# A two-layer trunk on one core: the diagonal products of the linear attention in another order, and two empty steps in its schedule

## The chip, the cores and the metric

The kernel runs on one core of one Trainium2 chip. The metric is the device time of one execution, in microseconds; lower is better. The core's engines work side by side and each takes its instructions in order: TensorE (PE in the profile, with its weight loads as PEld), VectorE (DVE), ScalarE (ACT), GpSimd (POOL), and SyncE (SP), which issues the DMA transfers.

## The reference

The input is a stream of 2064 tokens of 1024 channels (16 learned ones and 2048 given ones). Layer 0 is a gated convolution module, layer 1 gated linear attention; after each comes `h = LayerNorm(sqrt(2)·h + mixer(h))`. All is float32. Of layer 1, which the change touches:

```python
u = h @ w_in                       # q, k: 4 heads x 128;  v, r: 4 heads x 256;  a1: 16
glog = log_sigmoid(a1 @ w_a2 + b_a) / 16
# per head, in chunks; bc is the running sum of glog inside a chunk
att[t, s] = sum_d q[t,d] k[s,d] exp(bc[t,d] - bc[s,d])     for s <= t
o = att @ v + (q * exp(bc)) @ S
S = exp(b_last) * S + (k * exp(b_last - bc)).T @ v
o = o * rsqrt(mean(o*o) + 1e-6) * norm_g
y = (o * silu(r)) @ w_out
```

## The kernel before, in words

The program has four phases. Phases 1 and 2 are the convolution layer, phase 3 is the attention, phase 4 its output projection and the last LayerNorm. Wide matrix products are made as three float32r products of high and low parts (`mm3`, lines 102 to 108).

Phase 3 (`phase3`, line 798) works through four blocks of 512 tokens (the first also holds the 16 learned ones) and, in each, four heads. For each head two things are woven together.

- The **projections** (`proj_units`, line 555): k, q, v and the two halves of r, as TensorE products named `pj_b<block><k|q|v|r>`, with weights that SyncE fetches and ACT and DVE split. After each unit the generator yields its cost: 1 for a product of 512 columns by 128 channels (24 matmuls), 0.53 for each of four v chunks, 0.5 for the gates (`gates`, line 626, which end in the running sum `b` on DVE, line 643).
- The **attention** of the head (`gla_units`, line 651), a generator of steps between `yield`s: the decayed keys `kh` and queries; the transposes of the keys (`pk`, line 691); the levels m = 64, 32, 16 of the attention matrix (`att`, line 727) with the state updates (`ds`, lines 704 and 705); the levels 8, 4, 2 and 1, whose factors `A` are built by POOL, ACT and DVE (lines 717 to 721, 741 to 744); the diagonal products `sm` (lines 755 and 756); their masking, sum and split into `a_h` and `a_l` (lines 758 to 768); the outputs `o` (line 777); their norm; and the transposes of the outputs (`oT`, line 789), which leave for `og_d`.

The diagonal products are small. A head's block has four chunks of 128 tokens, taken two by two into one PSUM tile `sm`; each chunk has four blocks of 32 tokens at rows s = 0, 32, 64, 96. For each block there are four products with 128 rows of contraction: levels 8, 4 and 2, each 32 x 32, and one of 32 x 48 that holds level 1 and the diagonal. The rows s to s + 32 of the output fix which 32 columns of the array a product takes.

How many attention steps are run per projection unit is set by `GRATE` (line 40): `debt += GRATE * cost`, and one step for each whole unit of debt (lines 806 to 809). A head's steps run while the r of this head and the k, q and v of the next are projected: 2 + 1 + 0.5 + 1 + 4 x 0.53 = 6.62 units of cost. A head has 14 yields (15 in the first block). What is left of a head's steps is run out before the next head begins (lines 810 to 813). Steps and units only give the order in which the program is written: a scheduler then places the instructions on each engine by its own estimate of when they are ready, so their final order is not the written one.

Of the kernel before, what the change touches and what calls it, by code (L numbers as in the profile page):

```python
# [19 lines left out]
P = 128  # L20
# [16 lines left out]
NH = 4  # L37
TAU = 16.0
QSCALE = 128.0 ** -0.5
GRATE = 2.35  # L40
VCOST = 0.53
CB = 4
WRB = 3
# [6 lines left out]
class Trunk:  # L50
# [600 lines left out]
    def gla_units(self, h, hd, bi, t0, n):  # L651
        nc, K = self.nc, self
# [20 lines left out]
        bs, ks, qs = b[:, sl], k_[:, sl], q_[:, sl]  # L673
# [11 lines left out]
        nc.vector.tensor_tensor(kh, kh, ks, op=ALU.mult)  # L685
        nc.vector.tensor_tensor(ebf, ebf, qs, op=ALU.mult)
        qh, ql = self.pair3("q", eb, nc.gpsimd, nm)
        yield
        pt = self.pt.tile([P, 4, P], F32, tag="g", name=f"pk{nm}")
        for c in range(4):  # L690
# [20 lines left out]
        for m in (64, 32, 16, 8, 4, 2):  # L711
# [11 lines left out]
            if m >= 16:  # L723
                for c in range(4):
                    for s in range(0, P, 2 * m):
                        a = c * P + s
                        nc.tensor.matmul(
                            att[s : s + m, c, s + m : s + 2 * m],
                            lhsT=A[:, a : a + m],
                            rhs=A[:, a + m : a + 2 * m],  # L730
                            start=False,
                            stop=False,
                            skip_group_check=True,
# [4 lines left out]
        A1 = self.gp.tile([P, 16, 48], F32, tag="A1", name=f"A1{nm}", bufs=1)  # L738
# [8 lines left out]
        red = self.gp.tile([P, 4, 32], F32, tag="red", name=f"red{nm}")  # L747
        for c2 in range(2):
            sm = self.pt.tile([P, 2, 144], F32, tag="g", name=f"sm{nm}_{c2}")
            for c in range(2):  # L750
                for s in range(0, P, 32):
                    a = (2 * c2 + c) * P + s
                    w = slice(a, a + 32)
                    for i, m in enumerate((8, 4, 2)):
                        nc.tensor.matmul(sm[s : s + 32, c, 48 + 32 * i : 80 + 32 * i], lhsT=lv[m][:, w], rhs=lv[m][:, w], start=True, stop=True, skip_group_check=True)  # L755
                    nc.tensor.matmul(sm[s : s + 32, c, :48], lhsT=ks[:, w], rhs=A1[:, a // 32], start=True, stop=True, skip_group_check=True)
            ms = self.gp.tile([P, 2, 144], F32, tag="ms", name=f"ms{nm}_{c2}")
            nc.vector.tensor_tensor(ms, sm, K.lmask.unsqueeze(1).to_broadcast([P, 2, 144]), op=ALU.mult)
            rd = red[:, 2 * c2 : 2 * c2 + 2]
            nc.vector.tensor_reduce(rd, ms[:, :, 16:].rearrange("p c (l t) -> p c t l", t=32), axis=mybir.AxisListType.X, op=ALU.add)  # L760
            odd = rd.rearrange("p c (s u) -> p c s u", u=2)[:, :, :, 1]
            nc.vector.tensor_tensor(odd, odd, ms[:, :, :16], op=ALU.add)
            yield
# [2 lines left out]
            nc.vector.tensor_tensor(at[:, c], red[:, c].unsqueeze(1).to_broadcast([P, 4, 32]), K.blk, op=ALU.mult)  # L766
        nc.vector.tensor_tensor(at, at, att.rearrange("p c (a b) -> p c a b", b=32), op=ALU.add)
        ath, atl = self.pair3("a", at.rearrange("p c a b -> p c (a b)"), nc.gpsimd, nm, 1)
        yield
        osb = self.gp.tile([P, 4, 256], F32, tag="osb", name=f"osb{nm}", bufs=1)  # L770
        sq = self.gp.tile([P, 3, 4], F32, tag="sq", name=f"sq{nm}")
# [26 lines left out]
    def phase3(self, wo):  # L798
# [3 lines left out]
        for bi, h, cost, hd in self.proj_units():  # L802
            if bi > cur:
                cur = bi
                nb = self.block(bi + 1) if bi < last else self.load_half(wo, 0)
            debt += GRATE * cost
            while debt >= 1:
# [145 lines left out]
```

## Time and profile before

| | |
|---|---|
| median of 3 runs | 1757.4 us (1753.49 to 1759.08) |
| the profiled execution | 1755.36 us, of which its span is 1753.6 us |
| PE busy | 1702.3 us (97%), 11715 instructions |
| DVE busy | 1402.4 us (80%) |
| POOL, ACT busy | 944.3 us (54%), 842.9 us (48%) |
| granted TensorE clock, mean | 0.993 |

The span runs from the first instruction of the program to the last. A matmul's duration in the profile is its time through a pipeline, so the next one begins before it ends; what a product costs TensorE is the time from its start to the next start. A program matmul on plain float32 operands stands in the trace as two MATMUL records: the program has 1024 `sm` products, the trace 2048 records. The stretch from 820 to 1580 us holds the attention of all 16 heads.

### The profile page before, as it was taken

How to read it: one execution, taken by the hardware profiler on the slowest of the kernel's cores; microseconds unless marked ns; L12 is line 12 of the kernel's file. 1: busy time of each engine (PE TensorE's matmuls, PEld its weight loads, DVE VectorE, ACT ScalarE, POOL GpSimd, SP SyncE). 2: the span in 40 equal slices, each digit the busy share in tenths (PEclk: the TensorE clock that was granted, in tenths of full speed). 3: DMA queues.
4: the chain of work that ended last, by engine and by line, in shares of the span. 5: the costliest groups of instructions: out<-in, count | busy, mean ns of one | idle time of the engine just before them, and what ended most of it. 6: DMA issues, size and time to landing. Idle time of an engine off the chain costs nothing.

```text
span 1753.6 us, 29029 instructions
## 1 busy us (share of the span) xinstructions
PE 1702.3 (97%) x11715; PEld 1514.2 (86%) x11715; DVE 1402.4 (80%) x1869; ACT 842.9 (48%) x1269; POOL 944.3 (54%) x675
## 2 busy tenths in 40 slices
PE   8999999999998998999999999999999999999998
PEld 8999999999998776767888888888888878888886
DVE  5789999999998898777666687777878687887665
ACT  6445555655544454445455455555555455541000
POOL 0879999999975788756233233333333153331000
PEclk9999999999999999999999999999999999999999
DMA  7111111111256544433113222232223322354441
GB/s 244 37 37 37 37 69 40 73 56 54 75 169 217 173 162 139 140 124 99 67 61 109 87 92 78 84 105 79 85 85 96 111 73 85 123 165 162 147 135 62
DMA packets 103910, 178.72 MB, mean 102 GB/s; under 512 B 8624, under 2 KB 68400, under 8 KB 103776
## 3 DMA queue, kind: packets, MB, share of 16 engines
q1 hardware_dynamic: 103776, 176.86, 30.0%
q8 instruction: 92, 1.51, 0.4%
q14 instruction: 42, 0.34, 0.1%
HBM read 134.70 MB, written 42.14 MB: 101 GB/s over the span
## 4 chain that ended last, share of the span: by engine, by line
PE 72%; DVE 14%; POOL 5%; ACT 4%; issue 3%; DMA 2%; SPq 0%; DVEq 0%; POOLq 0%; ACTq 0%
PE pj_y L108 4%; PE pj_y L107 4%; PE pj_y L106 4%; PE pj_g L107 3%; PE pj_g L108 3%; PE pj_g L106 3%; PE pj_z L107 3%; PE pj_a L107 3%; PE pj_z L106 3%; PE pj_a L106 3%; PE pj_z L108 3%; PE pj_a L108 3%; PE sm L755 2%; DVE A L721 1%; DVE A L720 1%
## 5 line engine op out<-in xcount | busy, mean ns | idle before, releaser
L196 POOL TENSOR_TENSOR gacc<-gacc,prod 128x1024 f32<-128x1024 f32 (+1 forms) x156 | 385.9, 2477 | 65.2 <-ACT prod L195 56.2
L204 DVE SCALAR_TENSOR_TENSOR cacc<-glu,prm,cacc 128x1024 f32<-128x1024 f32 (+1 forms) x292 | 374.9, 1294 | 7.0
L717 POOL TENSOR_TENSOR A<-b 128x256 f32<-128x256 f32 x96 | 83.2, 867 | 292.1 <-DVE b L643 110.0
L195 ACT ACTIVATE prod<-glu,prm 128x1024 f32<-128x1024 f32 (+1 forms) x156 | 179.2, 1155 | 111.0 <-POOL gacc L196 110.8
L106 PE MATMUL pj_g<-xh,h_w 128*128 128x412 f32 (+1 forms) x320 | 114.2, 357 | 6.0 <-ACT h_w L73 4.2
L107 PE MATMUL pj_g<-xl,h_w 128*128 128x412 f32 (+1 forms) x320 | 114.0, 356 | 0.3 <-DVE xl L74 0.3
L108 PE MATMUL pj_y<-woh,l_gt 128*128 128x512 f32 (+1 forms) x272 | 108.3, 403 | 5.8 <-DVE l_gt L74 5.7
L108 PE MATMUL pj_g<-xh,l_w 128*128 128x412 f32 (+1 forms) x320 | 113.0, 354 | 0.0
L107 PE MATMUL pj_a<-xl,h_w 128*128 128x412 f32 (+1 forms) x320 | 112.4, 351 | 0.0
L106 PE MATMUL pj_a<-xh,h_w 128*128 128x412 f32 (+1 forms) x320 | 112.3, 351 | 0.0
L107 PE MATMUL pj_z<-xl,h_w 128*128 128x412 f32 (+1 forms) x320 | 112.3, 351 | 0.0
L106 PE MATMUL pj_z<-xh,h_w 128*128 128x412 f32 (+1 forms) x320 | 112.2, 351 | 0.0
L108 PE MATMUL pj_z<-xh,l_w 128*128 128x412 f32 (+1 forms) x320 | 112.0, 351 | 0.0
L108 PE MATMUL pj_a<-xh,l_w 128*128 128x412 f32 (+1 forms) x320 | 111.9, 350 | 0.0
L106 PE MATMUL pj_y<-woh,h_gt 128*128 128x512 f32 (+1 forms) x272 | 110.0, 407 | 1.3 <-ACT h_gt L73 1.2
L107 PE MATMUL pj_y<-wol,h_gt 128*128 128x512 f32 (+1 forms) x272 | 109.6, 403 | 0.0
L106 PE MATMUL pj_y<-w4h,h_g 128*128 128x512 f32 x256 | 99.6, 390 | 0.0
L108 PE MATMUL pj_y<-w4h,l_g 128*128 128x512 f32 x256 | 99.6, 390 | 0.0
L107 PE MATMUL pj_y<-w4l,h_g 128*128 128x512 f32 x256 | 99.6, 390 | 0.0
L654 ACT ACTIVATE A<-A 128x512 f32<-128x512 f32 (+1 forms) x112 | 66.7, 596 | 57.7 <-POOL A L718 56.4
L388 POOL TENSOR_TENSOR rs<-rs,mhalf 128x1 f32<-128x1 f32 x16 | 14.5, 905 | 145.8 <-DVE rs L387 145.8
L377 DVE SCALAR_TENSOR_TENSOR xt<-xt,pj_y 128x512 f32<-128x512 f32 (+1 forms) x66 | 44.5, 678 | 59.5 <-PE pj_y L108 59.4
(428 smaller groups left out, 5366.5 us busy)
## 6 DMA issues: line engine op xcount, KB each, us to landing
r_w<-w SPq DMA_DIRECT2D x24, 512.0 KB, 3.3
c<-c_d SPq DMA_DIRECT2D x16, 512.0 KB, 4.5
szb<-sz_d SPq DMA_DIRECT2D x16, 512.0 KB, 4.6
xt<-x_tok SPq DMA_DIRECT2D x16, 512.0 KB, 4.6
h_d<-xt SPq DMA_DIRECT2D x16, 512.0 KB, 2.8
r_h1b<-h_d SPq DMA_DIRECT2D x16, 512.0 KB, 3.9
og_d<-og SPq DMA_DIRECT2D x32, 256.0 KB, 3.4
xt<-h_d SPq DMA_DIRECT2D x16, 512.0 KB, 3.5
```

The source lines that it names most:

```text
L106: mm(out, lhsT=lh, rhs=rh, start=(i == 0), stop=False)
L107: mm(out, lhsT=lh, rhs=rl, start=False, stop=False)
L108: mm(out, lhsT=ll, rhs=rh, start=False, stop=(i == n - 1))
L195: nc.scalar.activation(pr, src(k), AF.Copy, scale=tap(k))
L196: nc.gpsimd.tensor_tensor(st["g"], st["g"], pr, op=ALU.add)
L204: nc.vector.scalar_tensor_tensor(out, src(k), tap(k), acc, op0=ALU.mult, op1=ALU.add)
L377: self.nc.vector.scalar_tensor_tensor(xt[:m, es], xt[:m, es], ALPHA, ps, op0=ALU.mult, op1=ALU.add)
L654: ex = lambda o, i: nc.scalar.activation(o, i, AF.Exp, scale=1.0 / TAU)
L717: nc.gpsimd.tensor_tensor(Av[:, :, 0], mid, bv[:, :, 0], op=ALU.subtract)
L720: nc.vector.tensor_tensor(Av[:, :, 0], Av[:, :, 0], kv[:, :, 0], op=ALU.mult)
L721: nc.vector.tensor_tensor(Av[:, :, 1], Av[:, :, 1], qv[:, :, 1], op=ALU.mult)
L755: nc.tensor.matmul(sm[s : s + 32, c, 48 + 32 * i : 80 + 32 * i], lhsT=lv[m][:, w], rhs=lv[m][:, w], start=True, stop=True, skip_group_chec ...
```

## The change

Three edits. The loops of the diagonal products are turned: for each level the four 32-row blocks come one after the other, in place of the four products of one block. Two `yield`s are added, each behind a `yield` that was there: one before the keys' transposes, one before the outputs, so a head has 16 steps (17 in the first block). `GRATE` goes from 2.35 to 2.7. Lines behind the first edit move by 2 to 5.

```diff
-GRATE = 2.35
+GRATE = 2.7
 ...
         qh, ql = self.pair3("q", eb, nc.gpsimd, nm)
+
+        yield
         yield
         pt = self.pt.tile([P, 4, P], F32, tag="g", name=f"pk{nm}")
 ...
             for c in range(2):
-                for s in range(0, P, 32):
-                    a = (2 * c2 + c) * P + s
-                    w = slice(a, a + 32)
-                    for i, m in enumerate((8, 4, 2)):
+                a = (2 * c2 + c) * P
+                blocks = [(s, slice(a + s, a + s + 32)) for s in range(0, P, 32)]
+                for i, m in enumerate((8, 4, 2)):
+                    for s, w in blocks:
                         nc.tensor.matmul(sm[s : s + 32, c, 48 + 32 * i : 80 + 32 * i], lhsT=lv[m][:, w], rhs=lv[m][:, w], start=True, stop=True, skip_group_check=True)
-                    nc.tensor.matmul(sm[s : s + 32, c, :48], lhsT=ks[:, w], rhs=A1[:, a // 32], start=True, stop=True, skip_group_check=True)
+                for s, w in blocks:
+                    nc.tensor.matmul(sm[s : s + 32, c, :48], lhsT=ks[:, w], rhs=A1[:, (a + s) // 32], start=True, stop=True, skip_group_check=True)
 ...
         ath, atl = self.pair3("a", at.rearrange("p c a b -> p c (a b)"), nc.gpsimd, nm, 1)
         yield
+        yield
         osb = self.gp.tile([P, 4, 256], F32, tag="osb", name=f"osb{nm}", bufs=1)
```

Nothing is added to or taken from any engine's work; the order on all five engines changes from the first head on. Three places, all on PE. In the names, `sm_3_1` is the second `sm` tile of head 3, `pj_b3v` a projection for block 3, and a trailing `x4` means four such rows in succession.

The first place is the second half of the diagonal products of head 3 in block 2. Before:

```order
L108 MATMUL ds_3_3_13320<-vhb2v_12923,k_l_3_13134 128x256
L106 MATMUL pj_b3v_3_13464<-h_b3v_0_13138,xhb_12753 128x272
L107 MATMUL pj_b3v_3_13464<-l_b3v_0_13139,xhb_12753 128x272
L108 MATMUL pj_b3v_3_13464<-h_b3v_0_13138,xlb_12754 128x272
L755 MATMUL sm_3_1_13427<-A_3_8_13293 32x32
L755 MATMUL sm_3_1_13427<-A_3_4_13299 32x32
L755 MATMUL sm_3_1_13427<-A_3_2_13305 32x32
L756 MATMUL sm_3_1_13427<-A_3_13311,b2k_12656 32x48
```

and now:

```order
L106 MATMUL pj_b3v_3_13464<-h_b3v_1_13135,xhb_12753 128x272
L758 MATMUL sm_3_1_13427<-A_3_8_13325 32x32 x4
L758 MATMUL sm_3_1_13427<-A_3_4_13331 32x32 x4
L758 MATMUL sm_3_1_13427<-A_3_2_13337 32x32 x4
L760 MATMUL sm_3_1_13427<-A_3_13343,b2k_12625 32x48 x4
```

The four levels of one block stood in a row, then came the next block; now the four blocks of one level stand in a row, and four such groups make a chunk.

The second place is the change of blocks, where the last head of block 2 gives its transposed outputs `oT_3` and head 0 of block 3 begins (`att_0`, `pk_0`), amid the r projection `pj_b3r`. Before:

```order
L789 MATMUL oT_3_1_13630<-ident,osb_3_13539 128x128
L789 MATMUL oT_3_0_13589<-ident,osb_3_13539 128x128 x3
L789 MATMUL oT_3_1_13630<-ident,osb_3_13539 128x128 x3
L108 MATMUL pj_b3r_0_13722<-xhb_12753,l_b3r_0_13640 128x512
L106 MATMUL pj_b3r_0_13722<-xhb_12753,h_b3r_0_13639 128x512
L107 MATMUL pj_b3r_0_13722<-xlb_12754,h_b3r_0_13639 128x512
L108 MATMUL pj_b3r_0_13722<-xhb_12753,l_b3r_0_13640 128x512
L106 MATMUL pj_b3r_0_13722<-xhb_12753,h_b3r_0_13639 128x512
L107 MATMUL pj_b3r_0_13722<-xlb_12754,h_b3r_0_13639 128x512
L108 MATMUL pj_b3r_0_13722<-xhb_12753,l_b3r_0_13640 128x512
L727 MATMUL att_0_13694<-A_0_32_13749 32x32 x2
L691 MATMUL pk_0_13685<-ident,kh_0_13676 128x128 x4
```

and now:

```order
L108 MATMUL pj_b3r_0_13692<-xhb_12753,l_b3r_0_13640 128x512
L729 MATMUL att_0_13728<-A_0_64_13730 64x64
L794 MATMUL oT_3_0_13589<-ident,osb_3_13539 128x128 x4
L794 MATMUL oT_3_1_13630<-ident,osb_3_13539 128x128 x4
L729 MATMUL att_0_13728<-A_0_64_13730 64x64 x2
L693 MATMUL pk_0_13719<-ident,kh_0_13676 128x128 x4
L729 MATMUL att_0_13728<-A_0_64_13730 64x64
L729 MATMUL att_0_13728<-A_0_32_13749 32x32 x8
```

Seven matmuls of `pj_b3r` that stood between the transposes `oT_3` and `pk_0` now stand ahead of `oT_3`; the level 32 of `att_0` has moved behind `pk_0`.

The third place is the first head of all, at its keys' transposes `pk_0`. Before:

```order
L727 MATMUL att_0_6879<-A_0_64_6881 64x64
L667 MATMUL dsm_6819<-vm_6509,ktm_6817 128x256
L727 MATMUL att_0_6879<-A_0_64_6881 64x64 x3
L106 MATMUL pj_b0k_0_6907<-xhb_6209,h_b0k_0_6837 128x264
L107 MATMUL pj_b0k_0_6907<-xlb_6210,h_b0k_0_6837 128x264
L108 MATMUL pj_b0k_0_6907<-xhb_6209,l_b0k_0_6838 128x264
L106 MATMUL pj_b0k_0_6907<-xhb_6209,h_b0k_0_6837 128x264
L691 MATMUL pk_0_6870<-ident,kh_0_6827 128x128 x4
```

and now:

```order
L729 MATMUL att_0_6879<-A_0_64_6881 64x64
L667 MATMUL dsm_6819<-vm_6509,ktm_6817 128x256
L729 MATMUL att_0_6879<-A_0_64_6881 64x64 x3
L729 MATMUL att_0_6879<-A_0_32_6900 32x32 x3
L693 MATMUL pk_0_6870<-ident,kh_0_6827 128x128 x4
L729 MATMUL att_0_6879<-A_0_32_6900 32x32 x5
L106 MATMUL pj_b0k_0_6930<-xhb_6209,h_b0k_0_6837 128x264
```

Four matmuls of the next head's k projection, `pj_b0k`, stood ahead of `pk_0` and now come behind it; three products of level 32 stand there instead.

## Rows read from the trace of the kernel before

**Rows 1.** The page's first section: engine, busy us, share of the span, instructions.
```profile
PE 1702.3 (97%) x11715; PEld 1514.2 (86%) x11715; DVE 1402.4 (80%) x1869; ACT 842.9 (48%) x1269; POOL 944.3 (54%) x675
```
**Rows 2.** By stage: us, busy of PE, PEld, DVE, ACT, POOL; clock, DMA.
```profile
820.00:1580.00 760.00, 740.16 (x6917) 640.99 (x6916) 581.98 (x994) 394.28 (x701) 269.69 (x287) 0.99 0.28 93
```
**Rows 3.** PE's waits from 820 to 1580 us: total us, times, longest.
```profile
PE pk L691 <- DVE kh L685: 3.9, 2, 3.2
PE o L106 <- ACT a_h L73: 3.8, 4, 1.2
PE trb L495 <- DVE xlb L498: 3.3, 2, 2.2
PE oT L789 <- DVE osb L784: 2.5, 4, 1.5
PE o L108 <- POOL a_l L74: 2.3, 2, 2.0
```
**Rows 4.** Busy time by stage, of instructions on tile sm alone.
```profile
820.00:1580.00 760.00, 53.00 (x2048) 46.11 (x2048) 14.40 (x32) 0.99 0.28 93
```
**Rows 5.** Timeline of PE, one half of a head: start us, us, engine, line.
```profile
1386.02 0.40 PE L755 MATMUL sm<-A 128*32 128x32 f32 x8
...
1387.49 0.39 PE L106 MATMUL pj_b3v<-h_b3v,xhb 128*128 128x272 f32 x1
```
**Rows 6.** Timeline of PE: four records of one 32-row block, and what follows.
```profile
1474.67 0.31 PE L755 MATMUL sm<-A 128*32 128x32 f32 x4
1474.91 0.50 PE L633 MATMUL pj_z<-ah,a 128*128 128x512 f32 x1
```
**Rows 7.** Timeline of PE: att products 32 wide, alternating between two column groups.
```profile
1512.07 0.32 PE L727 MATMUL att<-A 128*32 128x32 f32 x8
1512.32 0.39 PE L106 MATMUL ds<-vhb3v,k_h 128*128 128x256 f32 x1
...
935.14 0.45 PE L727 MATMUL att<-A 128*32 128x32 f32 x16
935.52 0.39 PE L106 MATMUL pj_b0k<-xhb,h_b0k 128*128 128x264 f32 x1
```
**Rows 8.** Timeline of PE: att products 16 wide, over all four column groups.
```profile
939.45 0.39 PE L727 MATMUL att<-A 128*16 128x16 f32 x32
939.77 0.39 PE L106 MATMUL pj_b0k<-xhb,h_b0k 128*128 128x264 f32 x1
```
**Rows 9.** Timeline of PE at the change to block 3; waits in brackets.
```profile
1414.67 0.40 PE L106 MATMUL pj_b3r<-xhb,h_b3r 128*128 128x512 f32 x1
1414.90 0.39 PE L107 MATMUL pj_b3r<-xlb,h_b3r 128*128 128x512 f32 x1
1416.78 0.44 PE L789 MATMUL oT<-ident,osb 128*128 128x128 f32 x2 [1.49 <-DVE osb L784]
...
1419.16 0.78 PE L108 MATMUL pj_b3r<-xhb,l_b3r 128*128 128x512 f32 x1
...
1420.16 0.63 PE L107 MATMUL pj_b3r<-xlb,h_b3r 128*128 128x512 f32 x1
1420.59 0.63 PE L108 MATMUL pj_b3r<-xhb,l_b3r 128*128 128x512 f32 x1
```
**Rows 10.** Timeline of DVE over the same change of blocks.
```profile
1415.38 2.96 DVE L784 TENSOR_SCALAR osb<-osb,sq 128x256 f32<-128x256 f32 x4
...
1419.40 0.68 DVE L685 TENSOR_TENSOR kh<-kh,b3k 128x512 f32<-128x512 f32 x1
```
**Rows 11.** Busy time and granted clock (PEclk) of three stretches.
```profile
831.10:837.90 6.80, 5.66 (x32) 5.42 (x32) 4.75 (x9) 1.65 (x4) 0.00 (x0) 0.50 0.44 154
1418.20:1421.60 3.40, 3.40 (x11) 2.81 (x12) 3.40 (x6) 1.00 (x2) 0.00 (x0) 0.50 0.27 90
1541.10:1544.50 3.40, 3.40 (x18) 3.40 (x17) 3.40 (x6) 0.00 (x0) 0.88 (x1) 0.50 0.00 0
```
**Rows 12.** A wait of POOL from 820 to 1580 us.
```profile
POOL kh L683 <- ACT kh L778: 74.2, 10, 9.8
```

## The prediction

> **What bounds the kernel now.** First the page's busy times: PE is busy 97% of the span, the next engine, DVE, 80% [rows 1]. Then the same by stage: the change acts on the attention, 820 to 1580 us, where PE is busy 740 of 760 us and DVE 582 [rows 2]. So TensorE bounds the stage, and work taken from it shortens the kernel as far as nothing else comes late. What comes late now is in PE's waits: about 20 us in 760, and all of it on DVE, ACT or POOL results for the keys' transposes `pk`, the outputs `o`, their transposes `oT` and the next block's input transposes `trb` [rows 3]. Last the diagonal products: 2048 records that hold PE for 53 us of the stage, counted from first start to last end [rows 4]. Those are the two sums that the change can touch.
>
> **Part 1: the diagonal products side by side.** A whole half of a head is 64 records and lasts from 1386.02 to 1387.49, 1.47 us to the start of the next work, or 23 ns a record [rows 5]. There are 32 halves: 47 us.
>
> What is one record worth if it stands alone? Four records of one block, all in the same 32 columns of the array, take 0.24 us [rows 6]. The `att` products of level 32 alternate between two column groups: 8 records take 0.25 us, 16 take 0.38 [rows 7]. The further 8, four in each group, cost 0.13 us, 32 ns for each record in its group; what is left of the 0.25 us, 0.12 us, is start and drain. One group alone gives (0.24 - 0.12)/4 = 30 ns. So a record keeps its own column group for about 31 ns, and a second group works beside it for nothing. A record 48 wide I put at 31 x 48/32 = 47 ns, an estimate.
>
> In before a block's eight records (48 of the 64 in a half are 32 wide, 16 are 48 wide) all go to one group before the next group is named. End to end a half would be 48 x 31 + 16 x 47 = 2.24 us; it takes 1.47 - 0.12 = 1.35, so 1.7 groups work at a time. In the new order the four groups are named in turn, with two records each. If all four run, a half takes a quarter of 2.24 us plus 0.12, 0.68 us, and saves 0.79; times 32, 25 us. The scheduler still cuts some halves with state updates, as it does now, and each cut pays the 0.12 again: I take **24 us**.
>
> The other bound: the only place where four groups are seen together is level 16 of `att`, 32 records in 0.32 us [rows 8], less 0.12 that is 6.2 ns a record. If this is a limit on starts, it is under the 8 ns (31/4) that I need, and nothing changes. If it is a limit on columns streamed, records twice as wide cost 12.5 ns and those of 48 columns 19: a half takes 48 x 12.5 + 16 x 19 + 120 ns = 1.02 us, and the saving is 14 us. I take the first, because the second group in [rows 7] costs nothing at all, and because 16-wide records in four groups need no explanation beyond their starts.
>
> The Trainium skill's page "TensorE: Matmul & The Clock Gate" (Part 1) speaks against the change: start to start never drops below about 25 ns, however few columns a matmul has. By that, an estimate from the page's figure, 2048 records would need 51 us in any order, and the saving would be nil. This trace does not agree: level 16 starts a record every 10 ns with its drain included [rows 8].
>
> **Part 2: the empty steps and the rate.** A head's 6.62 units now feed 17.9 steps instead of 15.6, for 16 instead of 14; the slack in units is 0.7 as before, so heads don't pile up. In the written order the stretch between the decayed keys and their transposes, and that between the split of `a` and the outputs, grows from 1/2.35 = 0.43 to 2/2.7 = 0.74 units. A unit is 24 matmuls of 0.23 us [rows 9], so each gets 1.7 us more cover. But the scheduler places the work, and the places shown in the order don't bear the cover out. At the first head `pk` loses four covering matmuls; the longest wait, 3.2 us for `kh` [rows 3], stays, since `kh` stands at the same place on DVE. At the change to block 3, seven matmuls (1.6 us) move ahead of `oT`, which shortens its waits (the first is 1.49 us [rows 9]), but `pk` now follows at once, and its `kh` ends at 1419.40 + 0.68 = 1420.08 on DVE, behind `osb` [rows 10]. Before, PE had `oT` behind it at 1419.16; the last wait just changes its name, for a gain of about 1 us.
>
> Three of the waits have a second price: the clock granted is half (1.2 GHz) in 13.6 us of the stage, each time in or right behind a wait on `pk`, `oT` or `o` [rows 11]; there a matmul takes 0.43 us in place of 0.23 [rows 9], so 6 us are lost. Bounds for part 2: all waits of `pk`, `o` and `oT` go, 12.5 us, with the 6; or the shifted order adds as many waits as the seven matmuls cost, 1.6 us, in five heads, 8 us. I take **3 us** gained: about one short wait in each of two or three heads, and one of the three half-clock stretches.
>
> **What is given back.** PE reaches each later point of a head 24/16 = 1.5 us earlier. Chains that PE itself starts behind the diagonal products (mask, sum, split, outputs) move along. Chains started ahead of them (the next head's gates, POOL's factors, and the `a_l` queued behind these) don't, and where one ends last already the 1.5 us is lost. [rows 3] names four waits for `a_h`, two for `a_l`: at half of the six, **4 us** given back; bounds 0 and half the saving, 12 us.
>
> **The sum.** -24 - 3 + 4 = -23 us. From the profiled execution's 1755.4 that is 1732.4; the median of the runs shown lies 2.0 above it, so 1734.
>
> **Rivals.**
> - *Columns, not starts, limit four groups.* Saving 14 in place of 24: 1757.4 - 14 - 3 + 4 = 1744. For it: no row shows four groups of 32 columns. Against it: [rows 7].
> - *The bound moves to the DVE chains.* DVE's 582 us in 737 is 79%, not a bound by itself, but its queue is in order, and half the saving can come back as longer rows of the kind in [rows 3]: 1757.4 - 24 + 12 = 1745.
> - *The waits go as well.* All of part 2's upper end, 18 us, with the 24 and 2 us given back: 1717. For it: the added steps stand exactly where PE waits. Against it: the order.
> - *A floor on starts.* If TensorE begins one such record in about 23 ns whatever the group, as [rows 5] alone would allow, part 1 is nil and part 2 leaves 1754 to 1758. Against it: [rows 8]. The Trainium skill's page "TensorE: Matmul & The Clock Gate" (Part 1) states such a floor.
> - *Slower, through the keys' buffer.* The squares of the outputs are written into `kh`, which has one buffer (lines 680 and 772); so POOL's next `kh` waits for them, 74.2 us already [rows 12], and the factors of levels 4 and 2 are queued behind it. Outputs that come 1.7 us later delay `kh`, `pk` and `sm` of the next head. While POOL is idle enough (270 of 760 us busy) it costs nothing; from the point where `sm` waits for its factors in every head it costs 16 x 1.7 = 27 us: 1734 + 27 = 1761.
>
> **How the numbers follow.** Forecast 0.60, with a range of its own of 1728 to 1741 (3 us of cuts and 4 us of waits either way); columns 0.13; DVE chains 0.10; waits go 0.08; floor 0.05; slower 0.04. The range 1725 to 1750 leaves out the last three, 0.17. A measurement of this kernel can tell 0.3%, 5.3 us, from no change, so faster is below 1752.1: the first four, 0.91, less 0.02 for a give-back beyond 12 us, 0.89; the same: the floor and a little of both neighbours, 0.07; slower 0.04.
>
> **What would show it.** Part 1: an unbroken half of `sm` in 0.65 to 0.75 us and `sm` busy near 29 us in place of 53; 1.0 us would mean columns, 1.4 the floor. Part 2: `pk` still waits about 3 us at the first head; waits of `pk`, `o` and `oT` together at 9 to 14 us; half-clock stretches of 7 to 14 us. Given back: DVE busy unchanged, the stage about 737 us long. Wrong would be a stage as long as now with short `sm` runs, which only new waits on PE could make.

## The result, and the profile after

The changed kernel takes 1736.7 us (median of 4 runs, 1735.0 to 1738.3), the kernel before 1755.5 beside it: a ratio of 0.989 [0.987, 0.992], 18.7 us faster. Forecast were 1734 us and 23 us less. On a second chip the same pair gave 1737.4 against 1754.8, 0.9905 [0.9891, 0.9919], 17.4 us. (Brackets behind a ratio are its 95% interval.)

TensorE is still the bound. The page's busy line of the changed kernel, to be read against [rows 1]:

```profile
PE 1679.1 (97%) x11715; PEld 1491.7 (86%) x11715; DVE 1396.5 (81%) x1869; ACT 841.4 (49%) x1269; POOL 938.4 (54%) x675
```

PE does 23.2 us less. The span is 1734.4 us, 19.2 shorter. So PE's idle time, span less busy, went from 51.3 to 55.3 us: 23.2 - 4.0 = 19.2. The same by stage, the attention of the changed kernel against [rows 2] (busy of PE, PEld, DVE, ACT, POOL; clock, DMA). The window was set 20 us shorter, so that it holds nearly the same number of PE's records, 6902 against 6917. Under it stand the diagonal products alone, against [rows 4] (PE, PEld, DVE):

```profile
820.00:1560.00 740.00, 714.92 (x6902) 615.28 (x6902) 573.73 (x983) 391.46 (x697) 262.02 (x285) 0.99 0.29 95
```
```profile
820.00:1560.00 740.00, 30.32 (x2048) 23.92 (x2048) 13.48 (x30) 0.99 0.29 95
```

The same 2048 records hold PE for 30.3 us in place of 53.0, and the stage's work ends some 20 us earlier. About 2 us of this lie ahead of the stage, in work whose order is the same in both kernels: PE's first record of `pj_b0v` starts at 783.33 us, before at 785.66. Nearly the whole fall of PE's busy time, 22.7 of 23.2 us, stands in the row of the products. One half of a head of the changed kernel that nothing cuts, on PE's timeline (start us, us, operation, records), against [rows 5]:

```profile
1375.01 0.40 PE L758 MATMUL sm<-A 128*32 128x32 f32 x24
1375.22 0.27 PE L760 MATMUL sm<-A,b2k 128*32 128x48 f32 x8
1375.31 0.38 PE L758 MATMUL sm<-A 128*32 128x32 f32 x23
1375.50 0.24 PE L760 MATMUL sm<-A,b2k 128*32 128x48 f32 x2
1375.51 0.20 PE L758 MATMUL sm<-A 128*32 128x32 f32 x1
1375.53 0.29 PE L760 MATMUL sm<-A,b2k 128*32 128x48 f32 x6
1375.74 0.39 PE L107 MATMUL pj_b3v<-l_b3v,xhb 128*128 128x272 f32 x1
```

From 1375.01 to the next start at 1375.74 are 0.73 us; before they were 1.47.

PE's longest waits in the stage, changed kernel, against [rows 3] (total us, times, longest us):

```profile
PE pk L693 <- DVE kh L685: 5.2, 3, 3.9
PE ds L106 <- DVE Sm L707: 4.7, 2, 3.2
PE o L106 <- ACT a_h L73: 4.0, 3, 2.5
PE o L106 <- ACT kh L783: 3.6, 4, 1.7
PE o L108 <- POOL a_l L74: 2.8, 4, 0.8
PE trb L495 <- DVE xlb L498: 1.5, 2, 1.1
PE oT L794 <- DVE osb L789: 0.9, 2, 0.4
```

Two waits of `o` in the kernel before, the next behind those of [rows 3]:

```profile
PE o L106 <- DVE xlb L498: 1.7, 1, 1.7
PE o L106 <- ACT kh L778: 1.5, 2, 0.8
```

The waits haven't shrunk, they have been dealt out anew. Those for `oT` fell from 2.5 to 0.9 us and those for `trb` from 3.3 to 1.5; `pk` rose from 3.9 to 5.2, the outputs' wait for the squares on ACT (named `kh`, since they are written there) rose from 1.5 to 3.6, and 4.7 us for the state (`ds` behind `Sm`) are new among the long ones. All idle time of PE in the stage is 740 - 714.9 = 25.1 us, against 19.8 before.

### The profile page after: what moved, and what is told of

Its sections match the earlier page's. It is cut to its first block, busy times and chain, and to the rows that moved or that the text cites. A ratio compares the mean times of both kernels' runs of the same rounds, so it can differ in the third digit from the quotient of the medians.

```text
span 1734.4 us, 29031 instructions
## 1 busy us (share of the span) xinstructions
PE 1679.1 (97%) x11715; PEld 1491.7 (86%) x11715; DVE 1396.5 (81%) x1869; ACT 841.4 (49%) x1269; POOL 938.4 (54%) x675
## 4 chain that ended last, share of the span: by engine, by line
PE 69%; DVE 12%; POOL 8%; ACT 5%; issue 3%; DMA 3%; SPq 0%; DVEq 0%; POOLq 0%; ACTq 0%
PE pj_y L106 4%; PE pj_y L108 4%; PE pj_y L107 4%; PE pj_g L107 3%; PE pj_g L108 3%; PE pj_g L106 3%; PE pj_z L107 3%; PE pj_z L106 3%; PE pj_a L107 3%; PE pj_a L106 3%; PE pj_z L108 3%; PE pj_a L108 3%; POOL A L720 1%; POOL A L719 1%; PE att L729 1%
```

## The experiments

All runs of a group ran on one chip beside the kernel before, except that the run with one group at a time went with the third group. Where a diff says so it is against the changed kernel, else against the kernel before.

**First group: the parts, and how many column groups work.** The products alone (the changed loops, rate and steps as before; against the changed kernel):

```diff
-GRATE = 2.7
+GRATE = 2.35
...
-        yield      # the added one ahead of pk
...
-        yield      # the added one ahead of o
```

> The kernel before with the turned product loops alone (GRATE 2.35, no added steps). Theory A (the gain is the products', and the steps with the rate cost about 3 us of it): 22 to 24 us below the kernel before, an unbroken half of the products near 0.73 us as in the changed kernel. Rival B (the products lose part of their saving to waits, and the added steps win it back): 12 to 16 us below. Rival C (steps and rate are nothing): 19 us below, as the changed kernel.

Measured: 1743.6 us, 0.9931 [0.9917, 0.9944], 11 us faster than the 1754.8 beside it. The products hold PE for 32.2 us, and an unbroken half takes 0.73 us as in the changed kernel. So 20.8 us are saved on the products, and only 11 arrive. Its waits on PE:

```profile
PE oT L790 <- DVE osb L785: 5.6, 7, 2.0
PE pk L691 <- DVE kh L685: 4.1, 2, 3.4
PE o L108 <- POOL a_l L74: 3.7, 6, 1.3
```

`oT` waits seven times in place of four, and `a_l` six in place of two [rows 3]: the short rows got more numerous, as the rival of the DVE chains has it. But these two rows grew by 4.5 us only, and PE's idle time in the whole span by 5.5, from 51.3 to 56.8. The rest of what doesn't arrive is busy time of PE outside the products: 1685.3 - 32.2 = 1653.1 us, before 1702.3 - 53.0 = 1649.3. The stretches of the attention at half clock add up to 17.0 us, before to 13.6 [rows 11].

The steps and the rate alone (the two added `yield`s and `GRATE`, the loops as before):

```diff
-GRATE = 2.35
+GRATE = 2.7
...
+        yield      # ahead of pk
...
+        yield      # ahead of o
```

> The kernel before with the two added steps and GRATE 2.7 alone, the products in the old order. Theory A: 2 to 5 us above the kernel before. Rival B: 3 to 7 us below. Rival C: within 2 us of it. In all three a half of the products stays at 1.47 us.

Measured: 1752.0 us, 0.9982 [0.9973, 0.9990], 2.8 us faster; `sm` busy 52.7 us, as before. By itself this part is worth what was forecast for it. Its share of the whole isn't that, though: in the same group the changed kernel stood at 1737.4, so that on top of the products the steps gave 1743.6 - 1737.4 = 6 us.

> The changed kernel once more, beside its parts on the same chip. All theories: 17 to 21 us below the kernel before. It gives the sum that the parts must make: A has products -23 and steps +3, B -14 and -5, C -19 and 0.

Measured: 1737.4 us, 0.9905 [0.9891, 0.9919]. Its profile repeats the first one: span 1734.3 us, PE busy 1679.2. Against the profile of the products alone its span is 7.8 us shorter: 1.9 in the products (30.3 us in place of 32.2; 13 halves of heads stand uncut, with the products alone 4), 4.2 in PE's other busy time, 1.7 in idle time. Of the attention 10.2 us run at half clock in place of 17.0. So what the steps add on top of the products is for the greater part shorter busy time and not shorter waiting.

Two groups at a time (two blocks in turn through all levels, then the other two; against the changed kernel, with rate and steps taken out as for the products alone):

```diff
-                a = (2 * c2 + c) * P
-                blocks = [(s, slice(a + s, a + s + 32)) for s in range(0, P, 32)]
+              a = (2 * c2 + c) * P
+              blocks4 = [(s, slice(a + s, a + s + 32)) for s in range(0, P, 32)]
+              for blocks in (blocks4[:2], blocks4[2:]):
                 for i, m in enumerate((8, 4, 2)):
                     for s, w in blocks:
...
```

> As e1_products_only, but the blocks of 32 rows are taken two by two: rows 0 and 32 alternate through all four levels, then rows 64 and 96. Theory A (a record keeps its own column group for about 31 ns, whatever the others do): with two groups at work a half takes about 2.24/2 + 0.12 = 1.24 us, a little less where the pairs overlap, so 6 to 9 us below the kernel before. Rival (what counts is that two neighbours differ in their group, and two groups give all there is to have): a half near 0.73 us, and the time of e1. Rival (a limit on columns streamed): a half at 1.0 to 1.1 us.

Measured: 1748.5 us, 0.9967 [0.9954, 0.9980], 6.2 us faster; `sm` busy 37.5 us. The first rows and the last of an unbroken half, and what follows:

```profile
1195.77 0.38 PE L756 MATMUL sm<-A 128*32 128x32 f32 x14
1195.98 0.21 PE L758 MATMUL sm<-A,b1k 128*32 128x48 f32 x1
1195.98 0.20 PE L756 MATMUL sm<-A 128*32 128x32 f32 x1
...
1196.49 0.27 PE L758 MATMUL sm<-A,b1k 128*32 128x48 f32 x4
1196.69 0.39 PE L107 MATMUL pj_b2v<-l_b2v,xhb 128*128 128x272 f32 x1
```

0.92 us, shorter than two groups that take turns strictly would need (2.24/2 + 0.12 = 1.24): when one pair's last records run, the other pair has begun. As the loops are written, a pair's 12 records of 32 columns are followed by its four of 48; in the rows 14 of 32 columns start first, two of them the other pair's.

One group at a time (the old rate, no added steps; all 16 records of a 32-row block of both chunks in succession):

```diff
-            for c in range(2):
-                for s in range(0, P, 32):
+            for s in range(0, P, 32):
+                for c in range(2):
                     a = (2 * c2 + c) * P + s
```

> The kernel before with the products of both chunks taken row block by row block: sixteen records in succession go to one column group before the next is named. Theory A (a record keeps its own group for about 31 ns; TensorE looks only a few records ahead): a half takes 1.8 to 2.2 us in place of 1.47, PE busy with sm about 63 to 70 us in place of 53, and 10 to 20 us above the kernel before. Rival (the order of the records is not what counts): 1.47 us as before.

Measured: one run of 1766.3 us, 11 slower than the 1755.3 of before beside it; `sm` busy 69.3 us. The first rows of a half, the rows at the first change of group, and the last:

```profile
1195.58 0.38 PE L755 MATMUL sm<-A 128*32 128x32 f32 x6
1195.79 0.25 PE L756 MATMUL sm<-A,b1k 128*32 128x48 f32 x2
1195.88 0.38 PE L755 MATMUL sm<-A 128*32 128x32 f32 x8
1196.07 0.21 PE L756 MATMUL sm<-A,b1k 128*32 128x48 f32 x1
1196.09 0.20 PE L755 MATMUL sm<-A 128*32 128x32 f32 x1
...
1197.16 0.35 PE L755 MATMUL sm<-A 128*32 128x32 f32 x6
1197.35 0.25 PE L756 MATMUL sm<-A,b1k 128*32 128x48 f32 x2
1197.53 0.33 PE L602 MATMUL at<-ident,a1x 128*128 128x128 f32 x1
```

1.95 us for 64 records. Inside one group a record of 32 columns takes 32 ns (the last six, 0.19 us from 1197.16 to 1197.35) and one of 48 takes 45 (two, 0.09 us from 1195.79 to 1195.88). End to end that would be 48 x 32 + 16 x 45 = 2.26 us, and 0.12 for the drain; the half is 0.43 us shorter, 0.14 at each of its three changes of group. At the first change the next group's records start between the last two of 48 columns (1196.07 and 1196.11).

The four orders of the same work, with nothing else changed by hand, each from one profiled execution:

| order of the products | half, us | `sm` busy | span | PE busy | PE idle |
|---|---|---|---|---|---|
| one group at a time | 1.95 | 69.3 | 1764.6 | 1717.6 | 47.0 |
| before: eight records, then the next group | 1.47 | 53.0 | 1753.6 | 1702.3 | 51.3 |
| two groups in turn | 0.92 | 37.5 | 1749.3 | 1691.8 | 57.5 |
| four groups in turn | 0.73 | 32.2 | 1742.1 | 1685.3 | 56.8 |

Two things follow. What a product costs is set by how many column groups the order names in turn. And from the first row to the last 37.1 us are taken from the products, of which 22.5 reach the span: 9.8 us return as idle time of PE, the other 4.8 as longer busy time elsewhere, partly at half clock (17.0 us of the attention in the last row, 13.6 in the first).

**Second group: which step does it, and which chain the waits hang on.** The first step with the products, then the second, each at a rate of 2.52 (against the changed kernel, the other `yield` taken out):

```diff
-GRATE = 2.7
+GRATE = 2.52
...
-        yield      # first kernel: the one ahead of o; second: the one ahead of pk
```

> The turned products with the first added step alone (before the keys' transposes) and GRATE 2.52, which is 2.35 x 15/14. Known so far against the kernel before: products alone -11 us, steps and rate alone -3, all together -17. Theory A (the cover of the outputs is what the products need, since the chain from the products to the outputs waits on DVE and POOL): here -11 to -13. Theory B (the cover of the keys' transposes is what counts): -15 to -18. Theory C (no step matters by itself, the scheduler's order is merely another one each time): anywhere between -9 and -18, and e8 likewise.

> The turned products with the second added step alone (before the outputs) and GRATE 2.52. Theory A: -15 to -18, with PE's waits for a_h, a_l and osb below the 12 us that they have with the products alone. Theory B: -11 to -13. Theory C: anywhere between -9 and -18.

Measured: 1743.6 us, 0.9937 [0.9925, 0.9948], and 1745.3 us, 0.9946 [0.9934, 0.9958], against 1755.1: 11.5 and 9.7 us faster, where the products alone gave 11. Neither step has a gain of its own here, as theory C has it, and PE's idle time is 59.4 and 62.9 us. The second shows where it goes, in the first row of PE's waits:

```profile
PE o L106 <- ACT kh L781: 11.8, 10, 1.7
```

The outputs wait ten times for ACT's squares of the outputs before them, which by the code read a PSUM tile that has to come free.

A scratch of their own for these squares, so that the next keys' buffer comes free earlier (against the changed kernel):

```diff
-        junk = kh[:, :256]
+        junk = at[:, 0:2].rearrange("p c a b -> p (c a b)")
```

> The changed kernel, with the squares of the outputs written into the tile at (free by then) in place of the keys' buffer kh, so that GpSimd's next kh no longer waits for them. Theory A (DVE's queue in order is what hands part of the saving back, kh comes late on DVE and not on GpSimd): within 3 us of the changed kernel. Rival (the shared buffer is what holds kh, the keys' transposes and the state back; PE's waits for pk, for ds and for the squares are 13 us in the changed kernel): 5 to 10 us below the changed kernel, so 22 to 28 below the kernel before.

Measured: 1746.5 us, 0.9949 [0.9934, 0.9963]: half of the gain is lost (the six runs spread from 1741.7 to 1748.6), and in the profiled execution, 1742.9 us, PE's idle time is 57.5 us. No theory expected that. POOL's `kh` no longer waits for the squares but for the gates' sum `b` on DVE, first the changed kernel, then this run:

```profile
POOL kh L683 <- ACT kh L783: 66.5, 9, 13.0
POOL kh L683 <- DVE b L643: 86.4, 9, 14.9
```

So in this order the buffer held back nothing that the gates wouldn't have. What ends PE's waits most is `a_l`:

```profile
PE o L108 <- POOL a_l L74: 7.2, 7, 1.6
```

The low parts of one weight split per head on POOL in place of DVE (16 instructions; against the changed kernel):

```diff
-        return self.load(..., self.nc.vector)
+        return self.load(..., self.nc.gpsimd if kind == "r1" else self.nc.vector)
```

> The changed kernel, with the low part of one weight tile in every head (the second half of r, 16 operations of 1.2 us) taken from DVE's queue and given to GpSimd, which is idle 65% of the attention. Theory A (DVE's queue hands back part of the saving): 3 to 8 us below the changed kernel. Rival (it is not DVE's load but the order and GpSimd's own queue): within 2 us of it or above it, with more waits for a_l.

Measured: 1747.7 us, 0.9955 [0.9943, 0.9967], 7.4 us faster than before, so again more than half of the gain is lost. DVE's busy time fell by only 1 us, to 1395.5, POOL's rose by 44, to 982.7, and the longest row is DVE's nevertheless:

```profile
PE oT L794 <- DVE osb L789: 9.3, 4, 4.3
```

DVE wasn't relieved: its 16 splits fewer are worth 19.9 us, but its other instructions took about 19 us longer, those of `osb` for one 31.0 us in place of 25.0, and on POOL a split takes 2.4 us in place of 1.3. So this run can't tell what a lighter DVE queue would give. Each of these edits also makes the scheduler place everything else anew. The first tells against the buffer as the cause; neither gives a price for one chain alone.

**Third group: the rate, or another order by chance.** The changed kernel at rates 2.6 and 2.85, and the products with rate 2.7 but without the steps:

```diff
-GRATE = 2.7
+GRATE = 2.6        # and 2.85
```

> The changed kernel with GRATE 2.6 in place of 2.7: the same steps and products, another order on every engine. Theory A (the products are worth about 21 us in every order, and what the waits take back depends on the order as a whole, 4 to 14 us in the runs so far): 8 to 17 us below the kernel before, TensorE's time for sm again 26 to 30 us, and the difference to the changed kernel found in PE's waits. Rival (the two steps together have a worth of their own, whatever the rate): 16 to 19 us below.

> The changed kernel with GRATE 2.85. Theory A: 8 to 17 us below the kernel before. Rival: 16 to 19 us below.

> The turned products with GRATE 2.7 and no added step: a head's 14 steps are fed 17.9, so they are written closer together and end earlier. Theory A: 5 to 15 us below the kernel before, as another order. Rival (the steps are what wins back): no better than 9 us below, with more waits for a_h, a_l and osb, since each chain has 0.37 units of cover in place of 0.43.

Measured, against 1755.3: 1739.2 us, 0.9908 [0.9895, 0.9922]; 1739.3 us, 0.9906 [0.9893, 0.9918]; without the steps 1749.0 us, 0.9965 [0.9952, 0.9978]. With both steps three rates, which give three orders, agree within 2 us, 16 to 17.5 us faster. Without them the gain is 11 at rate 2.35 and 6 at 2.7. That the last 5 to 6 us are one lucky order is unlikely by this: the two steps together give them at all three rates (at 2.35 they weren't run together). At the faster rate alone the waits for `a_h`, `a_l` and `osb` didn't grow as the rival had it (4.5 us in all, 12.4 with the products alone); it is again the outputs that wait for the squares, in PE's longest row:

```profile
PE o L106 <- ACT kh L779: 13.5, 12, 1.7
```

The same wait is 3.6 us in the changed kernel. No run beats the changed kernel.

## Why the prediction came out as it did

**What bounds the kernel: right.** PE stays at 97%, and time taken from it reaches the span, less what returns as waits and as longer work elsewhere.

**The products: right in mechanism and size.** Forecast 24 us, measured 22.7; forecast 0.68 us for a half, measured 0.73. The 31 ns for which a record keeps its column group, worked out from two differences in [rows 6, 7], and the 47 estimated for 48 columns stand in the open with one group at a time: 32 and 45 ns. The rival of the columns asked for 1.0 us a half, that of the floor for 1.4: both are refuted by the same row, 64 records in 0.73 us with their drain, 11.4 ns each. The Trainium skill's page "TensorE: Matmul & The Clock Gate" (Part 1) puts start to start at 25 ns or more; this trace doesn't agree where neighbours lie in different column groups, and inside one group a record takes 32.

**The steps and the rate: right alone, wrong as a term to be added.** Forecast 3 us, measured 2.8 alone, but 6 on top of the products. Reading the order gave the single places rightly. At the first head `pk` still waits, 3.9 us (before 3.2), and the clock is halved there as before. At the change to block 3, PE's timeline of the changed kernel, against [rows 9]:

```profile
1403.12 0.40 PE L108 MATMUL pj_b3r<-xhb,l_b3r 128*128 128x512 f32 x1
1403.45 0.33 PE L729 MATMUL att<-A 128*64 128x64 f32 x2
1404.21 1.55 PE L794 MATMUL oT<-ident,osb 128*128 128x128 f32 x8 [0.43 <-DVE osb L789]
1405.69 0.45 PE L729 MATMUL att<-A 128*64 128x64 f32 x4
1406.83 0.63 PE L693 MATMUL pk<-ident,kh 128*128 128x128 f32 x4 [0.69 <-DVE kh L685]
```

`oT` waits 0.43 us in place of 1.49, and the last wait is now that of `pk`, 0.69: the name has changed, as forecast. Busy time (of PE, PEld, DVE, ACT, POOL) and granted clock of three stretches of the changed kernel, against [rows 11]:

```profile
827.80:834.60 6.80, 4.48 (x27) 4.09 (x28) 6.80 (x12) 2.29 (x5) 1.37 (x2) 0.50 0.44 154
1404.00:1408.00 4.00, 3.10 (x34) 2.19 (x34) 4.00 (x8) 1.00 (x3) 0.21 (x2) 1.00 0.19 67
1517.30:1520.70 3.40, 3.40 (x17) 3.40 (x18) 2.73 (x4) 3.10 (x6) 3.40 (x5) 0.50 0.47 160
```

The first head's stretch at 0.50 (1.2 GHz) stays, that at the change to block 3 is gone, and the third row comes right behind a wait of `o`, 2.48 us for `a_h` ahead of 1517.15. The first and the third make 10.2 us in all, where 13.6 were before and 7 to 14 forecast.

**What is given back: the step that was mis-sized.** It said 4 us, from half of six waits at 1.5 us (which is 4.5). With the products alone the return is 20.8 - 11.1 = 10 us, close to the 12 that were its upper end and that made the rival of the DVE chains. The working looked only at chains that already ended last [rows 3], and only at waits. The runs show two parts in its place: 5.5 us of idle time, most of it in waits that weren't there (`oT` from 4 times to 7, `a_l` from 2 to 6), and about 4 us of PE's other work taking longer, with 17.0 us at half clock in place of 13.6. That the new waits are chains that had ended just in time, and come late once PE is 0.74 us earlier in each half, fits these rows; no run shows it chain by chain.

With the added steps, 22.7 - 18.7 = 4 us of the saving are missing in the end. The forecast had steps and return at 4 less 3, so it was off by 3 here and by 1.3 at the products; the 2.7 us of the median are less than the 4.3 that these make, because the kernel before ran 2 us lower beside it than in the runs that the forecast started from. That it came so close is in part luck: the return was 6 us larger than forecast, and the steps took back twice the 3 us that they were put at, for the greater part by shorter busy time, where the forecast had counted on waits above all.

Nor was it foreseen that `ds` would wait for the state. PE, DVE and POOL of the changed kernel at the longest such wait:

```profile
1054.82 0.28 PE L108 MATMUL pj_b1v<-h_b1v,xlb 128*128 128x256 f32 x1
1058.27 0.39 PE L106 MATMUL ds<-vhb1v,k_h 128*128 128x256 f32 x1 [3.16 <-DVE Sm L707]
```
```profile
1054.94 1.48 DVE L722 TENSOR_TENSOR A<-A,b1k 128x256 f32<-128x256 f32 x1
1056.34 1.48 DVE L723 TENSOR_TENSOR A<-A,b1q 128x256 f32<-128x256 f32 x1
1057.75 0.47 DVE L707 SCALAR_TENSOR_TENSOR Sm<-Sm,el,ds 128x256 f32<-128x256 f32 x1
1058.14 0.41 DVE L722 TENSOR_TENSOR A<-A,b1k 128x256 f32<-128x256 f32 x1
```
```profile
1054.70 1.43 POOL L74 TENSOR_TENSOR a_l<-at,a_h 128x512 fp32r<-128x512 f32 x1
1056.10 1.44 POOL L74 TENSOR_TENSOR q_l<-eb,q_h 128x512 fp32r<-128x512 f32 x1
```

Two factors `A` stand ahead of the state's update in DVE's queue, and each takes 1.48 us while POOL splits.

**Waits of `pk`, `o` and `oT`: missed.** Forecast 9 to 14 us together, measured 5.2 + 4.0 + 3.6 + 2.8 + 0.9 = 16.5. The forecast started from 12.5 us, the rows of these names in [rows 3]; with the two shorter rows of `o` before, shown above, it was 15.7, so these waits didn't fall at all. The window of the stage is 740 us long, forecast 737; since its length was chosen to match the work, that is no finding of its own.

**The slower rival: not seen.** The keys' buffer didn't slow the kernel; and since a scratch of their own for the squares costs 9 us rather than gaining any, the buffer isn't seen to hold the changed kernel either, in the one other order that was run.

**What stays open** is why one step alone brings nothing on top of the products, and why freeing the buffer or moving the splits loses half of the gain. The profiles say where the time lies, not why. With either step alone the half-clock time of the attention is 10.2 us, as in the changed kernel, but PE's idle time is 59.4 and 62.9 us in place of 55.1; with no step it is 56.8, and half-clock time and busy time are longer. In each kernel with the new products the waits wander between `o`, `oT`, `pk` and `ds`, with PE idle for 55 to 63 us in the whole span; no run held the order of all engines fixed while it changed one chain.

## What to carry to other kernels

Small matmuls that use a part of the array's columns should name the column groups in turn: the price of one in its group, and the gain of a second group beside it, can be read from places of the same trace where runs differ in length and in groups. Of time taken from the bounding engine count a share as returning (here about a quarter as its idle time), and look for it also in chains that may end just in time, which no row of waits shows yet, and in stretches at half clock. Slack in the written order and shorter work aren't independent terms: give the slack after the work has become shorter, and measure them together.

## What the runs showed of the hardware

The same DVE multiply of 128x256 float32 (line 723) takes 0.41 us, as the next `A` rows at 1058.14 do for line 722, and up to 1.52 us beside POOL's splits. In the rows above POOL's splits end at 1056.13 and 1057.54 us, DVE's multiplies at 1056.42 and 1057.82, each 0.28 to 0.29 us later. The changed kernel has 192 multiplies of lines 722 and 723; all 91 of them that take over 0.7 us end 0.28 to 0.29 us behind the end of a POOL instruction. This looks like a wait for POOL's instruction and not like a slower stream. The Trainium skill's page "SBUF — State Buffer" (SBUF: two separate sides) says that DVE instructions with two inputs in SBUF and GpSimd's share a port pair which one holds for its whole instruction while the other is blocked; the rows agree. By the traces, records of different column groups don't start in the order in which TensorE is given them. In the kernel before, the order of a block is three products of 32 columns and one of 48, six records and two, but [rows 5] begin with eight of 32. That a pair of groups begins while the last records of the other pair still run was expected only as "a little less" than 1.24 us a half; it took 0.92.
